# The three attention products in the order v, k, q, and the FFN's weight tiles shifted in steps of 16 bytes

## The chip, the core and the metric

The kernel runs on one core of a Trainium2 chip. The metric is device time in microseconds (us), the median of several executions. In a core, TensorE (PE) multiplies matrices, VectorE (DVE) and ScalarE (ACT) work element by element, GpSimd (POOL) does small vector work and issues some of the transfers, and SyncE (SP) issues most of the other transfers (DMAs). Each engine takes its instructions in its own order and waits on semaphores for the others. On PE each matmul needs its stationary operand loaded first; the profile lists that load as an instruction of its own, LDWEIGHTS, on a row PEld.

## What is computed

One layer of a streaming encoder, for 512 tokens of width 1024, in float32:

```python
h = rms_norm(x, norm_mix)
proj = h @ w_in                       # 8192 columns
u_pool, u_lru, q, k, v, g_logits = split(proj)
gates = sigmoid(g_logits + b_gate)    # three gates of 1024 columns
y_pool = pool_mixer(u_pool, ...); y_lru = rglru_mixer(u_lru, ...)
q = rms_norm(q per head, q_norm); k = rms_norm(k per head, k_norm)
y_sb = stick_breaking_attention(q, k, v)
merged = sum(gates[b] * (y[b] @ w_branch[b]) for b in range(3))
x = x + merged @ w_out
h2 = rms_norm(x, norm_ffn)
x = x + (silu(h2 @ w_ffn_gate) * (h2 @ w_ffn_up)) @ w_ffn_down   # 2816 wide
```

For this change it matters that q and k are normalised per head and that v is not.

## The kernel before

**Precision.** Each float32 operand is split into a high part, rounded to the matmul's format, and a low part, the rest. A product is then three matmuls: high by high, high by low, low by high. For weights, ACT writes the high part (a copy) and DVE the low part (a subtraction) of a tile of 128 x 1024; PE can't begin a product before both are there. `split_w` (lines 97 to 103) does it, with the tiles from `weight_tiles` (lines 93 to 95): tags `whi` and `wlo` of the pool `wp`, three buffers each. A weight tile has 1024 + 128 columns, of which a slice of 1024, beginning at column `o`, is used.

**Order.** The weight steps of the whole kernel, up to the FFN, stand in a list, `specs`, in the order in which PE will need them. `weights(key)` (lines 219 to 224) emits steps until up to three are ready, with a raised priority, so splits are made ahead of PE by as much as the three buffers allow. Work that follows a product (additions, norms, stores) goes to a list `bg`; `tick()` runs an entry of it after each part of a product.

**Startup** (lines 347 to 391). `WARM` small matmuls on a constant run on PE while the first data come. The small vectors `vt` are loaded by ACT's queue; the first tiles of x and the first halves of the first weight tile, `raw0`, are loaded by SP's queue in turn. Then PE multiplies the first gate columns (line 625).

**The stretch of q, k and v** (lines 718 to 765). Each of the three is a product of 512 tokens by 1024 columns with depth 1024, done by a scheme with seven block products in place of eight (`ORDER`: 11, 12, S2, S1, S3, S4, 22). Each block product is two halves of 12 matmuls with 512 moving columns (line 712), each with its own weight step of 128 x 1024. Eight of the fourteen weight steps of q, k or v also need a sum or difference of raw weight blocks on DVE (`qkv_sum`, line 150, by the table `SUMS_AT`). A snapshot (ACT, line 724) and an addition (DVE, line 727) make each of four result tiles, `r`, which `post` (lines 678 to 687) takes further. For q and k, `post` squares the tile (ACT, line 682), sums it per head (DVE, line 683) and puts `post2` on the list. `post2` (lines 689 to 701) computes the inverse root with `rsqrt` (lines 252 to 260: a power on POOL, then four small instructions on DVE), scales k's tile by it on ACT (eight copies, line 698) or, for q, writes the negated factor for later (line 700), and stores the tile with POOL's queue to the tensor `qd` in DRAM (line 675). For v, `post` only stores it.

The order is q (t = 0), k (t = 1), v (t = 2). Half chunks of the third gate, 24 matmuls each with one weight step, are placed after six of the block products by the table `AFTER`: after 12, S3 and 22 of q and after the same three of k. The last pieces of the recurrent mixer (inputs, scans and stores of its chunks 2 and 3, lines 601 to 614) are put on the list after q's S3.

After this stretch comes the pooling mixer together with the attention, head by head: `head_tasks` loads q, k and v of a head from `qd` by SP's queue (line 889), and PE transposes q and k (line 896).

**The FFN.** The first two of eleven chunks of the gate and up products are done directly, with 512 moving columns. The other nine (c = 2 to 10) use the seven-product scheme with 256 moving columns: each block product is 24 matmuls (`product`, lines 1176 to 1182). Six of eleven blocks of the down product are then done directly, and last come two halves of its output (c = 11 and 12) by the seven-product scheme again, 24 matmuls each block product. `make_a` (lines 1162 to 1174) makes the weight tiles for c = 2 to 12, three block products ahead. All of them lie at column `OFF` = 16 of their tile, so 64 bytes further in than the tiles of all other stages, which lie at column 0.

In the FFN the weight slice is the stationary operand and the activations are the moving one; in the stretch of q, k and v it is the other way round.

Of the kernel before, what the change touches and what calls it, by code (L numbers as in the profile page):

```python
# [25 lines left out]
QSCALE = float(HD) ** -0.5  # L26
NEG = -1.0e30
EARLY = 300
WARM = 8
GBUFS = 27  # L30
NDIRECT = 2
KD = 4
H = S // 2
AHEAD = 200
PAD = 96
OFF = 16
NAW, NAT, NAB = 8, 8, 13
NSP = 42
NLD = 12
# [24 lines left out]
def layer_kernel(ctx: ExitStack, tc: tile.TileContext, x, xt, vecs, w_in, w_pool, w_rg, w_ig,  # L64
                 w_branch, w_out, w_fg, w_fu, w_fd, out):
    nc = tc.nc
# [14 lines left out]
    def b4(shape, name, tag="b", dt=F32):  # L81
        bufs = {"w": NAW, "t": NAT, "b": NAB}[tag]
        return pools["ap0"].tile([P] + shape, dt, tag=tag, name=name, bufs=bufs)
# [5 lines left out]
    def cols(ap, k0, nk, c0, nc_):  # L89
        return ap[k0 * P:(k0 + nk) * P, c0:c0 + nc_].rearrange("(k p) c -> p k c", p=P)  # L90


    def weight_tiles(nh, nl, o=0):
        return [wp.tile([P, 1024 + 128], F32R, tag=tag, name=n)[:, o:o + 1024]
                for tag, n in (("whi", nh), ("wlo", nl))]
# [20 lines left out]
    def add_gate(br, c):  # L116
        add_chunk256(("gate", br, c), w_in, 5120 + br * 1024 + c * 256)
# [14 lines left out]
    WITH = {"11": "11", "12": "21", "S2": "T2", "S1": "T1", "S3": "T3", "S4": "22", "22": "T4"}  # L132
    CH = {"11": 0, "12": 0, "21": 1, "22": 1}
    KH = {"11": 0, "12": 1, "21": 0, "22": 1}
    qraw = {}

    def qkv_raw(t, nm, i):
        if (t, nm, i) not in qraw:
            qraw[t, nm, i] = r = b4([2, 512], f"qw{t}{nm}{i}", "w")
            nc.sync.dma_start(r, cols(w_in, 4 * KH[nm] + 2 * i, 2, 2048 + t * 1024 + CH[nm] * 512, 512))  # L140
        return qraw[t, nm, i]
# [15 lines left out]
    def add_seven(t, nm, i):  # L157
        def make(n):
            p = 2 * ORDER.index(nm) + i
            if p < 4:  # L160
                qkv_raw(t, nm, i)
            h, l = None, None
            if p == 1:
                h, l = split_w(qraw[t, nm, i], [P, 2, 512], n)
            if p in SUMS_AT:
                qkv_sum(t, *SUMS_AT[p])
            return (h, l) if h is not None else split_w(qraw[t, nm, i], [P, 2, 512], n)
        specs.append((("seven", t, nm, i), make))


    AFTER = {}
    for n, (t, nm) in enumerate(((0, "12"), (0, "S3"), (0, "22"), (1, "12"), (1, "S3"), (1, "22"))):
        AFTER[t, nm] = divmod(n, 2)

    for n in range(4):
        add_direct(("first", n), cols(w_in, 2 * n, 2, 5120, 512), 2, 512)
# [2 lines left out]
    for n in (0, 1, 2, 4, 3, 5, 6, 7):  # L179
        if n < 4:  # L180
            add_lru(n)
        else:
            add_gate(1, n - 4)
    for t in range(3):
        for nm in ORDER:
            add_seven(t, nm, 0)
            add_seven(t, nm, 1)
            if (t, nm) in AFTER:
                c, half = AFTER[t, nm]
                add_direct(("gate", 2, c, half), cols(w_in, 4 * half, 4, 7168 + c * 256, 256), 4, 256)  # L190
# [41 lines left out]
    vt = cst.tile([P, NV], F32, tag="vt", name="vt")  # L232
# [102 lines left out]
    with ExitStack() as first:  # L335
# [11 lines left out]
        wps = pb.tile([P, 2, S], F32, tag="mm", name="warm_ps")  # L347
        for i in range(WARM):
            nc.tensor.matmul(wps[:, 0, :], warm[:, 0:P], warm, start=True, stop=True)
# [7 lines left out]
        def load_xt(k):  # L357
            nc.sync.dma_start(xts[k], xt[k * P:(k + 1) * P, :])
# [12 lines left out]
        raw0 = wp.tile([P, 2, 512], F32, tag="raw", name="raw0")  # L371
        ready["first", 0] = hi0, lo0
        src0 = cols(w_in, 0, 2, 5120, 512)
        nc.scalar.dma_start(vt, vecs)
        for k in range(2):
            load_xt(k)
            nc.sync.dma_start(raw0[:, k, :], src0[:, k, :])
            dve.tensor_copy(hi0[:, k, :], raw0[:, k, :])
            dve.tensor_tensor(lo0[:, k, :], raw0[:, k, :], hi0[:, k, :].bitcast(F32), ALU.subtract)
            make_h(k)  # L380
# [239 lines left out]
        for k in range(KT):  # L620
            if k % 2 == 0:
                wh, wl = weights("first", k // 2)
# [51 lines left out]
        def store(t, i, j, r):  # L674
            nc.gpsimd.dma_start(rows(t, i, j), r)


        def post(t, i, j, r):
            if t < 2:
                sq = b4([2, 512], f"sq{t}{i}{j}")  # L680
                s_ = cst.tile([P, 8], F32, tag="ssq", name=f"ssq{t}{i}{j}", bufs=2)
                act(sq, r, AF.Square)
                dve.tensor_reduce(s_, sq.rearrange("p a (b d) -> p (a b) d", d=HD), AX.X, ALU.add)
                dve.tensor_scalar(s_, s_, 1.0 / HD, EPS, ALU.mult, ALU.add)
                bg.append(lambda: post2(t, i, j, r, s_))
            else:
                store(t, i, j, r)

        def post2(t, i, j, r, s_):

            y = cst.tile([P, 8], F32, tag="krs", name=f"krs{i}{j}", bufs=2) if t else \
                qrs[:, 0, 2 * j:2 * j + 2, 4 * i:4 * i + 4]
            y3 = y.rearrange("p (a b) -> p a b", a=2) if t else y
            rsqrt(y3, s_.rearrange("p (a b) -> p a b", a=2), (2, 4), f"q{t}{i}{j}")
            if t:
                v = r.rearrange("p a (b d) -> p (a b) d", d=HD)
                for n in range(8):
                    act(v[:, n, :], v[:, n, :], AF.Copy, scale=y[:, n:n + 1])
            else:
                dve.tensor_scalar(qrs[:, 1, 2 * j:2 * j + 2, 4 * i:4 * i + 4], y3, -1.0, None, ALU.mult)  # L700
            store(t, i, j, r)

        def tok_product(t, nm, ps, first):
            bh, bl = BQ[WITH[nm]]
# [10 lines left out]
                    tick()  # L715

        gate2 = {}
        for t in range(3):
            ps = {}
            r = {}  # L720

            def snap(key, src):
                r[key] = b4([2, 512], f"r{t}{key[0]}{key[1]}")
                act(r[key], src, AF.Copy)

            def final(key, src):
                dve.tensor_tensor(r[key], r[key], src, ALU.add)
                bg.append(lambda t=t, key=key, v=r[key]: post(t, *key, v))

            def bank(nm):  # L730
                ps[nm] = pb.tile([P, 2, 512], F32, tag="mm", name=f"ps_q{t}{nm}")
                return ps[nm]

            for nm in ORDER:
                if nm in ("11", "12", "S1", "22"):
                    bank(nm)
                dst = {"S2": "11", "S3": "11", "S4": "S1"}.get(nm, nm)
                tok_product(t, nm, ps[dst], dst == nm)
                if nm == "11":
                    snap((0, 0), ps["11"])  # L740
                elif nm == "12":
                    final((0, 0), ps["12"])
                elif nm == "S2":
                    snap((0, 1), ps["11"])
                elif nm == "S1":
                    snap((1, 1), ps["S1"])
                elif nm == "S3":
                    final((1, 1), ps["11"])
                    snap((1, 0), ps["11"])
                elif nm == "S4":  # L750
                    final((0, 1), ps["S1"])
                else:
                    final((1, 0), ps["22"])
                if (t, nm) == (0, "S3"):
                    for f, c in ((lru_input, 3), (lru_scan, 2), (lru_scan, 3), (lru_store, 2), (lru_store, 3)):
                        step(of(f, c))
                if (t, nm) in AFTER:
                    c, half = AFTER[t, nm]
                    if half == 0:
                        gate2[c] = chunk_psum(("gate", 2, c), pb)  # L760
                    half_chunk(gate2[c], ("gate", 2, c), half, hn, 1)
                    if half == 1:
                        gate_store(2, c, gate2[c], True)
# [258 lines left out]
    with ExitStack() as ffn:  # L1022
# [21 lines left out]
        for c in range(4):  # L1044
# [5 lines left out]
            for j in range(2):  # L1050
                k = 2 * c + j
                if c % 2 == 0:
                    x1p[c // 2, j] = mp.tile([P, 2, S], F32, tag="m", name=f"x1{c}{j}")
                t = x1p[c // 2, j][:, c % 2, :]
# [77 lines left out]
        CH = {"11": 0, "12": 0, "21": 1, "22": 1}  # L1132
        KH = {"11": 0, "12": 1, "21": 0, "22": 1}

# [4 lines left out]
        made = [0, NDIRECT]  # L1139

        def load_a(c):
            for nm in ("11", "21", "22", "12"):
                raw[c, nm] = t = corner([2, 4, P], f"w{c}_{nm}")
                for w in range(2):
                    if c < DOWN:
                        ap, c0 = (w_fg, w_fu)[w], c * 256
                    else:
                        ap, c0 = w_fd, (c - DOWN) * 512 + w * 256
                    nc.sync.dma_start(t[:, w], cols(ap, KH[nm] * 4, 4, c0 + CH[nm] * P, P))

# [11 lines left out]
        def make_a(upto):  # L1162
            while made[0] < min(upto, len(steps)):
                c, nm = steps[made[0]]
                made[0] += 1
                while made[1] < min(c + 2, DOWN):
                    load_a(made[1])
                    made[1] += 1
                sums_a(c, nm)
                h, l = (t.rearrange("p (w k c) -> p w k c", w=2, k=4)  # L1170
                        for t in weight_tiles(f"wh{c}_{nm}", f"wl{c}_{nm}", OFF))
                act(h, raw[c, nm], AF.Copy)  # L1172
                dve.tensor_tensor(l, raw[c, nm], h.bitcast(F32), ALU.subtract)  # L1173
                A[c, nm] = h, l
# [76 lines left out]
        for m in range(4):  # L1251
            t = fp.tile([P, 2, S], F32, tag="mm", name=f"ps_d{m}")
# [38 lines left out]
        for kc in range(KD, last + 1):  # L1291
            split_act(kc + 1)
            ah, al = split.pop(kc)
            for e in range(2):
                wh, wl = weights("fd", e, kc)
                if kc == last:
                    make_a(steps.index((DOWN, "11")) + e + 1)
                for j in range(4):
# [5 lines left out]
                    if kc == last:  # L1304
                        t = x1[m]
# [8 lines left out]
        for q in range(2):  # L1314
            c = DOWN + q
# [54 lines left out]
```

## Time and profile before

| | us |
|---|---|
| median of 3 executions | 939.15 |
| lowest, highest of them | 937.56, 939.16 |
| the profiled execution, its own time | 938.85 |
| its span, first to last instruction | 937.0 |

The profile gives busy time per engine, the chain of work that ended last, groups of instructions by line and shape, the waits and who ended them, and instructions in order of time. A row of the timeline has the start in us from the span's start, the duration in us (for a merged row the whole stretch), the engine, the line and the operation, and in brackets the idle time before it and who ended it. In the groups, the last two numbers ahead of the bar's right side are the total busy time in us and the mean duration of one in ns. In the windows, each row is a stretch of time; after its length come the busy time and, in brackets, the count of instructions of each engine, then the granted clock of TensorE as a share of the full one.

TensorE is busy for 99% of the span, VectorE for 76%, ScalarE for 52%. The mean granted clock is 0.998.

### The profile page before, as it was taken

How to read it: one execution, taken by the hardware profiler on the slowest of the kernel's cores; microseconds unless marked ns; L12 is line 12 of the kernel's file. 1: busy time of each engine (PE TensorE's matmuls, PEld its weight loads, DVE VectorE, ACT ScalarE, POOL GpSimd, SP SyncE). 2: the span in 40 equal slices, each digit the busy share in tenths (PEclk: the TensorE clock that was granted, in tenths of full speed). 3: DMA queues.
4: the chain of work that ended last, by engine and by line, in shares of the span. 5: the costliest groups of instructions: out<-in, count | busy, mean ns of one | idle time of the engine just before them, and what ended most of it. 6: DMA issues, size and time to landing. Idle time of an engine off the chain costs nothing.

```text
span 937.0 us, 13039 instructions
## 1 busy us (share of the span) xinstructions
PE 925.5 (99%) x5090; PEld 796.5 (85%) x5090; DVE 709.8 (76%) x890; ACT 489.6 (52%) x660; POOL 45.2 (5%) x69
## 2 busy tenths in 40 slices
PE   9999999899999999999999999999999999999998
PEld 6888778787878888788888888889999999988898
DVE  6797889777696699866865545699888888787465
ACT  6545997545655465644643234454554555653232
POOL 2000000222121000000000000000000000000000
PEclk9999999999999999999999999999999999999999
DMA  9484351652714934155532344355533334523001
GB/s 333 124 286 135 113 180 68 211 171 68 247 58 145 281 117 130 61 166 173 153 91 90 98 136 149 91 143 141 144 91 97 106 105 138 165 97 105 1 29 63
DMA packets 126894, 124.13 MB, mean 132 GB/s; under 512 B 7408, under 2 KB 105712, under 8 KB 126832
## 3 DMA queue, kind: packets, MB, share of 16 engines
q1 hardware_dynamic: 122800, 109.07, 38.2%
q0 software_dynamic: 3888, 14.16, 4.4%
q8 instruction: 40, 0.66, 0.3%
q14 instruction: 22, 0.18, 0.1%
q10 hardware_dynamic: 144, 0.06, 0.0%
HBM read 107.02 MB, written 16.25 MB: 132 GB/s over the span
## 4 chain that ended last, share of the span: by engine, by line
PE 82%; DVE 8%; ACT 5%; issue 3%; POOL 2%; DMA 0%; POOLq 0%; DVEq 0%; ACTq 0%
PE ps_y L1182 11%; PE ps_x L1182 8%; PE ps_br L227 5%; PE ps_br L229 5%; PE ps_br L228 5%; PE ps_q L712 3%; PE ps_d L227 3%; PE ps_d L228 3%; PE ps_d L229 3%; PE ps_gate L625 3%; PE ps_dy L1182 2%; DVE wlo L102 2%; PE ps_gate L227 2%; PE ps_gate L228 2%; PE ps_gate L229 2%
## 5 line engine op out<-in xcount | busy, mean ns | idle before, releaser
L101 ACT ACTIVATE whi<-raw 128x1024 fp32r<-128x1024 f32 x93 | 98.4, 1058 | 149.1 <-PE ps_br L228 46.2
L102 DVE TENSOR_TENSOR wlo<-raw,whi 128x1024 fp32r<-128x1024 f32 x93 | 113.5, 1221 | 63.8 <-ACT whi L101 58.6
L1172 ACT ACTIVATE wh_S<-w_S 128x1024 fp32r<-128x1024 f32 x44 | 46.6, 1061 | 56.6 <-PE ps_y L1182 25.6
L1173 DVE TENSOR_TENSOR wl_S<-w_S,wh_S 128x1024 fp32r<-128x1024 f32 x44 | 53.6, 1221 | 12.8 <-ACT wh_S L1172 12.6
L1172 ACT ACTIVATE wh<-w 128x1024 fp32r<-128x1024 f32 x33 | 35.0, 1062 | 49.0 <-issue 12.9
L102 DVE TENSOR_TENSOR wlo<-qw,whi 128x1024 fp32r<-128x1024 f32 x36 | 43.9, 1220 | 17.3 <-ACT whi L101 17.2
L1173 DVE TENSOR_TENSOR wl<-w,wh 128x1024 fp32r<-128x1024 f32 x33 | 40.3, 1222 | 17.4 <-ACT wh L1172 17.4
L101 ACT ACTIVATE whi<-qw 128x1024 fp32r<-128x1024 f32 x36 | 37.9, 1055 | 26.1 <-PE ps_q L712 17.6
L227 PE MATMUL ps_gate<-HH,whi 128*128 128x512 f32 x128 | 50.1, 392 | 0.0
L229 PE MATMUL ps_gate<-HH,wlo 128*128 128x512 f32 x128 | 49.9, 390 | 0.0
L228 PE MATMUL ps_gate<-HL,whi 128*128 128x512 f32 x128 | 49.8, 389 | 0.0
L227 PE MATMUL ps_d<-ah,whi 128*128 128x512 f32 x112 | 43.7, 391 | 0.0
L228 PE MATMUL ps_d<-al,whi 128*128 128x512 f32 x112 | 43.6, 389 | 0.0
L229 PE MATMUL ps_d<-ah,wlo 128*128 128x512 f32 x112 | 43.6, 389 | 0.0
L1160 DVE TENSOR_TENSOR w_S<-w,w 128x1024 f32<-128x1024 f32 x22 | 26.9, 1223 | 3.4 <-PE ps_d L228 2.9
L229 PEld LDWEIGHTS ps_gate<-HH,wlo 128*128 128x128 f32 x128 | 24.0, 188 | 5.3 <-DVE wlo L102 0.4
L227 PEld LDWEIGHTS ps_gate<-HH,whi 128*128 128x128 f32 x128 | 24.0, 188 | 5.2 <-issue 0.4
L228 PEld LDWEIGHTS ps_gate<-HL,whi 128*128 128x128 f32 x128 | 24.0, 188 | 4.9
L1160 DVE TENSOR_TENSOR w_S<-w,w_S 128x1024 f32<-128x1024 f32 x22 | 26.9, 1223 | 0.6
L933 DVE TENSOR_TENSOR_SCAN E<-K,zero 128x511 f32<-128x511 f32 (+3 forms) x32 | 25.5, 812 | 1.1 <-ACT K L928 1.1
L227 PE MATMUL ps_br<-yph,whi 128*128 128x512 f32 x64 | 25.6, 400 | 0.0
L227 PE MATMUL ps_pool<-HH,whi 128*128 128x512 f32 x64 | 25.6, 400 | 0.0
(634 smaller groups left out, 3015.7 us busy)
## 6 DMA issues: line engine op xcount, KB each, us to landing
raw<-in_w_in_dram SPq DMA_DIRECT2D x39, 512.0 KB, 4.9
qw<-in_w_in_dram SPq DMA_DIRECT2D x24, 512.0 KB, 4.7
raw<-in_w_branch_dram SPq DMA_DIRECT2D x24, 512.0 KB, 3.5
w<-in_w_ffn_gate_dram SPq DMA_DIRECT2D x36, 256.0 KB, 3.8
w<-in_w_ffn_up_dram SPq DMA_DIRECT2D x36, 256.0 KB, 4.2
raw<-in_w_ffn_down_dram SPq DMA_DIRECT2D x14, 512.0 KB, 3.5
qd<-r POOLq DMA_DIRECT2D x12, 512.0 KB, 3.4
at<-qd SPq DMA_DIRECT2D x24, 256.0 KB, 5.5
```

Of the source, the lines that this page charges most:

```text
L101: act(hi, raw, AF.Copy)
L102: dve.tensor_tensor(lo, raw, hi.bitcast(F32), ALU.subtract)
L227: nc.tensor.matmul(ps, lh, rh, start=start, stop=False, skip_group_check=skip)
L228: nc.tensor.matmul(ps, lh, rl, start=False, stop=False, skip_group_check=skip)
L229: nc.tensor.matmul(ps, ll, rh, start=False, stop=stop, skip_group_check=skip)
L625: nc.tensor.matmul(pss[n // 2][n % 2], w[:, k % 2, n * P:(n + 1) * P], hu[k][x_], start=k == 0 and w is wh and x_ == 0, stop=k == KT - 1 a ...
L712: nc.tensor.matmul(ps[:, a, :], b_[:, k, ts_], a_[:, kk, :], start=first and n == k == 0, stop=n == 2 and k == 3, skip_group_check=True)
L933: dve.tensor_tensor_scan(E[:, f - 1:c0 + n - 1][:, ::-1], K[:, f:c0 + n][:, ::-1], zero[:, 0:1].to_broadcast([P, c0 + n - f]), 1.0, ALU.mu ...
L1160: dve.tensor_tensor(t, raw[c, x], raw[c, y], op)
L1172: act(h, raw[c, nm], AF.Copy)
L1173: dve.tensor_tensor(l, raw[c, nm], h.bitcast(F32), ALU.subtract)
L1182: nc.tensor.matmul(o, a[:, w, k, :], b[:, k, :], start=first and n == k == 0, stop=n == 2 and k == 3, skip_group_check=True)
```

## The change

1. The three products run in the order v, k, q (`VKQ`), both in the list of weight steps and in the loop that issues the matmuls.
2. The half chunks of the third gate come after v's 12, S3 and 22, after k's 12, and after q's 11 and S2. The last pieces of the recurrent mixer come after v's S3.
3. `post` stores q's tile at once, like v's; only k's tile is stored in `post2`, after its scaling.
4. At the start `vt` is loaded by SP's queue, ahead of the first tile of x, and the first half of `raw0` by ACT's queue; `WARM` is 7 in place of 8.
5. In the FFN's seven-product parts the column at which a weight tile lies depends on the chunk and on the block product's place in it. For c = 3 to 6 it is 16 throughout, as before. For c = 2, 7, 8, 11 and 12 it is 0, 4, 8, 12, 16, 16, 16. For c = 9 and 10 it is 0, 124, 120, 116, 112, 112, 112. Four columns are 16 bytes.

```diff
-WARM = 8
+WARM = 7
...
-OFF = 16
+
+
+HELD, DOWNWARDS, UPWARDS = (16,) * 7, (0, 4, 8, 12, 16, 16, 16), (0, 124, 120, 116, 112, 112, 112)
+OFFS = {2: DOWNWARDS, 7: DOWNWARDS, 8: DOWNWARDS, 9: UPWARDS, 10: UPWARDS, 11: DOWNWARDS, 12: DOWNWARDS}
...
+    VKQ = (2, 1, 0)
...
-    for n, (t, nm) in enumerate(((0, "12"), (0, "S3"), (0, "22"), (1, "12"), (1, "S3"), (1, "22"))):
-        AFTER[t, nm] = divmod(n, 2)
+    for n, (t, nm) in enumerate(((0, "12"), (0, "S3"), (0, "22"), (1, "12"), (2, "11"), (2, "S2"))):
+        AFTER[VKQ[t], nm] = divmod(n, 2)
...
-    for t in range(3):
+    for t in VKQ:
         for nm in ORDER:
...
-        nc.scalar.dma_start(vt, vecs)
+        nc.sync.dma_start(vt, vecs)
         for k in range(2):
             load_xt(k)
-            nc.sync.dma_start(raw0[:, k, :], src0[:, k, :])
+            (nc.sync if k else nc.scalar).dma_start(raw0[:, k, :], src0[:, k, :])
...
-            else:
+            if t != 1:
                 store(t, i, j, r)
...
                     act(v[:, n, :], v[:, n, :], AF.Copy, scale=y[:, n:n + 1])
+                store(t, i, j, r)
             else:
                 dve.tensor_scalar(qrs[:, 1, 2 * j:2 * j + 2, 4 * i:4 * i + 4], y3, -1.0, None, ALU.mult)
-            store(t, i, j, r)
...
-        for t in range(3):
+        for t in VKQ:
...
-                if (t, nm) == (0, "S3"):
+                if (t, nm) == (VKQ[0], "S3"):
...
+                o = OFFS.get(c, HELD)[made[0] % 7]
...
-                        for t in weight_tiles(f"wh{c}_{nm}", f"wl{c}_{nm}", OFF))
+                        for t in weight_tiles(f"wh{c}_{nm}", f"wl{c}_{nm}", o))
```

## The prediction

> **What bounds the kernel now.** The page's first part comes first, then the windows view over the stretches that the change touches.
>
> ```profile
> PE 925.5 (99%) x5090; PEld 796.5 (85%) x5090; DVE 709.8 (76%) x890; ACT 489.6 (52%) x660; POOL 45.2 (5%) x69
> ```
>
> ```profile
> 148.57:207.39 58.82, 56.27 (x241) 46.16 (x240) 48.22 (x57) 30.86 (x33) 14.63 (x12) 0.97 0.54 179
> 207.39:263.18 55.79, 54.98 (x241) 44.90 (x240) 40.47 (x56) 31.75 (x45) 11.65 (x7) 1.00 0.42 132
> 263.18:301.84 38.66, 38.55 (x170) 31.31 (x168) 29.48 (x32) 22.40 (x35) 6.99 (x8) 1.00 0.29 100
> ...
> 148.57:176.90 28.33, 25.78 (x115) 21.03 (x113) 26.77 (x29) 17.12 (x19) 7.35 (x6) 1.00 0.38 130
> 176.90:180.40 3.50, 3.50 (x8) 2.79 (x9) 2.45 (x4) 0.00 (x0) 0.00 (x0) 0.51 0.86 264
> ```
>
> TensorE's own pace is the bound: it idles 11.5 us in all. The first three windows are q, k and v. They hold 2.55, 0.81 and 0.11 us of TensorE idle time, 3.5 together, and the last window a second loss: right after the longest wait, 8 matmuls took 3.5 us at a granted clock of 0.51. At full clock the spacing is:
>
> ```profile
> 605.92 0.39 PE L227 MATMUL ps_fu<-h2h,whi 128*128 128x512 f32 x1
> ...
> 616.80 0.39 PE L227 MATMUL ps_fg<-h2h,whi 128*128 128x512 f32 x1
> ```
>
> 48 matmuls lie between, so 10.88 / 48 = 0.2267 us each. Eight would take 1.81, so the low clock cost 1.7 us. All that a new order can win in q, k and v is thus 3.5 + 1.7 = 5.2 us. Who ended the waits, from the waits view of that stretch, and then the timeline up to the longest of them:
>
> ```profile
> DVE qrs L257 <- POOL rsqq L256: 6.4, 4, 1.8
> DVE krs L257 <- POOL rsqq L256: 5.3, 4, 1.9
> ...
> PE ps_q L712 <- DVE wlo L102: 2.5, 1, 2.5
> ...
> PE ps_q1S L712 <- DVE wlo L102: 0.8, 2, 0.5
> ```
>
> ```profile
> 165.81 1.19 DVE L683 TENSOR_REDUCE ssq<-sq 128x8 f32<-128x1024 f32 x1
> ...
> 168.31 3.69 POOL L256 TENSOR_TENSOR rsqq<-ssq,mhalf 128x8 f32<-128x8 f32 x1 [3.66 <-DVE ssq L684]
> ...
> 172.04 0.17 DVE L257 TENSOR_TENSOR qrs<-rsqq 128x8 f32<-128x8 f32 x1 [1.56 <-POOL rsqq L256]
> ...
> 173.31 1.22 DVE L610 TENSOR_TENSOR_SCAN li<-lt,ls 128x512 f32<-128x512 f32 x1
> ...
> 175.64 1.20 DVE L102 TENSOR_TENSOR wlo<-qw,whi 128x1024 fp32r<-128x1024 f32 x1
> ...
> 176.89 0.29 PEld L712 LDWEIGHTS ps_q<-wlo,hT3h 128*128 128x128 f32 x1 [2.97 <-DVE wlo L102]
> ```
>
> The reader is to see a queue on VectorE. The low weight part that TensorE wants stands behind the mixer's scans, and these behind an instruction of q's norm, L257, which holds VectorE idle for 1.56 us until POOL's power is done.
>
> **Part 1: v first.** v has no norm. Ahead of the wait at 176.9 VectorE then loses the reduction (1.19), the idle time (1.56) and the six small instructions of one norm. The small ones in that stretch, quoted by the 0.17 of L257, make about 6 x 0.17 = 1.0. Together 3.75 us, more than the 2.5 that TensorE waited. The scans stay where they were, after the first product's S3. So the wait goes, and with it the low clock behind it: -2.5 - 1.7 = **-4.2 us**. ScalarE also loses the square there. If only the scans decided, nothing would be gained; VectorE was busy 26.77 of 28.33 us in that window, so 3.75 us less is enough.
>
> The two waits of 0.8 us fall at k's S1, while VectorE still does q's last norms. Behind v there are none. I take half of it: **-0.4** (bounds -0.8 and 0).
>
> **Part 2: k and q with fewer gate chunks between.** A third of the stretch without gate halves is 38.55 us of TensorE for 168 matmuls (third window), and a gate half 24 x 0.2267 = 5.4. k keeps one of three: 38.6 + 5.4 = 44.0 us. VectorE's share, by the groups of k's window:
>
> ```profile
> L102 DVE TENSOR_TENSOR wlo<-qw,whi 128x1024 fp32r<-128x1024 f32 x12 | 14.7, 1222 | 7.3 <-ACT whi L101 7.3
> L683 DVE TENSOR_REDUCE ssq<-sq 128x8 f32<-128x1024 f32 x4 | 4.9, 1217 | 0.9 <-ACT sq L682 0.9
> ```
>
> 14 + 1 weight splits, 8 sums and 4 additions of the same 128 x 1024 size are 27 x 1.22 = 32.9; 4 reductions 4.9; 20 small ones at 0.17 3.4: 41.2 us. The waits on POOL add (6.4 + 5.3) / 8 x 4 = 5.9. 47.1 against 44.0: VectorE falls 3.1 us behind over k. What hides that is the lead: three weight buffers let it be two halves ahead, 2 x 12 x 0.2267 = 5.4 us, and in v's part it has 54.9 us of TensorE time for 17 splits, 8 sums, 4 additions (35.4) and about 10 of scans, so it enters k with the lead full. q then gets two gate halves near its beginning, 49.4 us for 41.2 + 1.2 + 0.7 + 5.9 = 49.0, level. The bounds are 0 (the lead covers it) and 3.1 + 1.7 = 4.8 (it doesn't, and one wait is long enough for the low clock). Bunched sums will cost something; I take **+0.8**, nearer the covered end, as k's window with as much of norms waited only 0.8.
>
> q last also puts q's norms ahead of the attention. Its stores no longer stand behind the norm (`post` issues them), but POOL is in order, so one can stand behind an earlier norm's power (3.69 us above at the longest). The first head's loads:
>
> ```profile
> 297.18 7.26 SPq L108 DMA_DIRECT2D raw<-in_w_in_dram  x3
> 304.61 1.48 SPq L889 DMA_DIRECT2D at<-qd  x3
> ```
>
> ```profile
> 296.31 0.73 POOL L675 DMA_DIRECT2D qd<-r  x1 [4.71 <-DVE r L727]
> ```
>
> SP's queue reaches them at 304.61 because of the weight loads ahead, over 8 us after the S4 result of the last third is stored now (296.31), so a store later by 3.7 us still lands. Bounds 0 and +2; I take **+0.2**. k's store moves past nothing, and v's and q's loads only change places in SP's queue with equal sizes.
>
> **Part 3: the start.**
>
> ```profile
> 0.74 0.40 ACTq L374 DMA_DIRECT2D vt<-in_vecs_dram  x1
> ...
> 0.74 0.40 SPq L358 DMA_DIRECT2D xt<-in_xt_dram  x1
> ...
> 1.19 0.44 SPq L377 DMA_DIRECT2D raw<-in_w_in_dram  x1
> ...
> 1.46 3.60 PE L349 MATMUL warm_ps<-warm 128*128 128x512 bf16 x8 [1.46 <-DVE warm L241]
> ...
> 3.92 0.72 ACT L364 ACTIVATE hu<-xt,vt 128x512 fp32r<-128x512 f32 x1 [1.16 <-DMA xt<-in_xt_dram]
> ...
> 5.35 0.42 DVE L378 CAST whi<-raw 128x512 fp32r<-128x512 f32 x1
> ...
> 5.91 2.05 PE L625 MATMUL ps_gate<-hu,whi 128*128 128x512 f32 x4 [0.86 <-DVE whi L378]
> ```
>
> x's first tile is issued 0.45 us later (behind `vt`), the weights 0.45 earlier. The first matmul waits for both; the cast ends at 5.77 and was itself behind VectorE's work on x. If the cast now goes ahead, the matmul starts up to 0.7 earlier; if not, 0.45 later. Those first matmuls are slow (4 in 2.05 us, against 0.91 at full pace), so an earlier start wins fewer full-pace matmuls than its length: **-0.2** (bounds -0.5 and +0.5). The eight warm-up matmuls end at 5.06, so one fewer ends ahead of the earliest start, 5.2.
>
> **Part 4: the FFN's offsets.** No transfer and no instruction is added; the same matmuls read from other columns.
>
> ```profile
> 638.72 2.83 PE ps_y L1182 x24
> ...
> 813.97 2.83 PE ps_y L1182 x24
> ```
>
> ```profile
> L228 PE MATMUL z<-qkl,qkh 128*128 128x256 f32 x16 | 4.7, 292 | 0.0
> L229 PE MATMUL py<-wth,vl 128*128 128x256 f32 x16 | 4.5, 284 | 0.0
> ...
> L228 PE MATMUL py<-wtl,vh 128*128 128x256 f32 x16 | 4.5, 282 | 0.0
> L229 PE MATMUL z<-qkh,qkl 128*128 128x256 f32 x16 | 4.5, 279 | 0.0
> ...
> L1182 PE MATMUL ps_y<-B011h,wh 128*128 128x256 f32 x5 | 1.4, 281 | 0.0
> ```
>
> A block product is 24 matmuls in 2.83 us, 117.8 ns each, and the chain shows this for every block product of c = 2 to 10. All of them hold 64 bytes of offset, so the rows say nothing of 0 to 48 bytes but this: z and py have the same width with no offset, and their mean durations are 279 to 292 ns against 281. 7 chunks have 4 block products at a new offset, 7 x 4 x 24 = 672 matmuls. Upper bound: + 11 ns x 672 = +7.4 us. Lower bound: half of a 512-column spacing, 113.3, so -4.5 x 672 = -3.0 us; and if the pace reached in steps then holds in all 1848 matmuls of this kind, -8.3. The nearest row, py, is 3 ns over for offset 0; between 0 and 64 bytes I take +1 ns on average, **+0.7**.
>
> The Trainium skill, page "TensorE: Matmul & The Clock Gate", Part 2, "Step-by-step: what each phase is for", says that the moving operand and the weight load come by two independent read ports, so that neither takes bandwidth from the other. By that rule the distance between them changes nothing, this term is 0 and the edit doesn't do what it says; the spread of 279 to 292 ns at one width is not decisive, since z and py also wait.
>
> **The sum** against the profiled execution's 938.85 (span 937.0, 1.85 around it): -4.2 - 0.4 + 0.8 + 0.2 - 0.2 + 0.7 = -3.1, so **935.8**; that execution lies 0.3 under the median of 939.15. Less than 0.2% of the time, 1.9 us, can't be told from no change.
>
> **The rivals.** (a) *A faster pace sets in with the steps.* For it: 117.8 is more than half of a 226.7 spacing, so there is something to lose per matmul. Against it: 1512 matmuls of c = 2 to 10 show one pace without exception, whatever precedes them. Time: 935.8 - 0.7 - 8.3 = 926.8, or 929.9 if only the seven stepped chunks have it (7 x 168 x 4.5 = 5.3). The same page, "Back-to-back issue gap", gives N / 2.4 + 2.5 ns for a single matmul, 109 ns here; by that estimate all 1848 would win 16 us, of which no row shows a sign. (b) *The intermediate offsets collide,* the other side. Place: the first four block products of the seven chunks; price 11 ns on 672 matmuls, +7.4, and +0.7 drops out: 942.5. It decides from 6 ns on (4.0 us over 672), where parts 1 to 3 are eaten up. For it: z's 292; against it: py's 282 to 284. (c) *VectorE can't carry k with one gate half.* Place: k's S3 to 22, where two gate halves are gone; price 4.8 us in place of 0.8: 939.8; a second such wait in q's last four products, where no gate half is left, 3 more: 942.8. For it: 47.1 against 44.0; against it: the lead of 5.4. (d) *v first doesn't remove the wait,* as the scans alone suffice to hold the weights back: 4.2 less gain, 940.0.
>
> **How the numbers follow.** Forecast 0.46 (933 to 938), (a) 0.20, (b) 0.14, (c) 0.12, (d) 0.08. Faster by over 0.2%, under 937.3: (a) and nine tenths of the forecast, 0.61. Within 0.2%: the rest of the forecast, two thirds of (d) and a part of (c), 0.14. Slower: 0.25. The range 927 to 942.5 leaves out the deepest of (a) and the far ends of (b) and (c), each below a tenth.
>
> **What would show it.** Part 1: no wait over 1 us on VectorE's `wlo` in the first third of the stretch, and a granted clock of 1.00 throughout. Part 2: waits on `wlo` under 1 us in all in k and q. Part 3: first matmul of line 625 at 5.2 to 5.9 us. Part 4: 2.83 us for 24 matmuls at 64 bytes, within 0.07 of it at the steps. The prediction is wrong if block products with HELD columns take another time than 2.83, if the clock drops in k or q, or if TensorE waits for q at the first transposes.

## The result and the profile after

| | before | changed |
|---|---|---|
| median, four executions each | 938.44 us | 926.89 us |
| lowest and highest | 937.56, 939.16 | 926.75, 929.27 |
| ratio, with its 95% interval | | 0.9883 (0.9864 to 0.9903) |
| profiled execution, its span | 938.85, 937.0 | 929.27, 927.1 |

Executions of either kernel differ by some 1.5 to 2.5 us with how fast the first dozen matmuls run (last section), so like is compared with like: when both were run again side by side, the lowest three are 937.10, 937.12 and 937.24 before, and 926.54, 926.72 and 926.73 changed, 10.4 to 10.6 us apart.

Where it came from, by windows cut at the first matmuls of the q, k, v stretch, of the nine FFN chunks and of the two down halves, and at the first matmuls that follow them (the prediction's windows of q, k and v begin 1.8 us later). The columns are the window, its length, then busy time and count of each engine, the granted clock, the DMA share and GB/s. First before:

```profile
146.76:300.02 153.26, 149.80 (x649) 122.37 (x648) 118.76 (x142) 86.70 (x113) 33.17 (x26) 0.99 0.42 139
638.56:816.64 178.08, 178.08 (x1514) 178.08 (x1513) 150.02 (x138) 97.55 (x120) 0.00 (x0) 1.00 0.41 119
890.24:932.64 42.40, 42.40 (x348) 41.76 (x347) 26.75 (x29) 12.74 (x12) 0.00 (x0) 1.00 0.10 36
```

The same after the change:

```profile
146.94:294.15 147.21, 147.21 (x650) 121.54 (x648) 115.89 (x129) 86.19 (x112) 23.01 (x24) 1.00 0.44 143
632.85:807.25 174.40, 174.40 (x1513) 174.40 (x1512) 149.60 (x138) 97.79 (x120) 0.00 (x0) 1.00 0.43 122
880.90:922.82 41.92, 41.92 (x349) 41.28 (x347) 26.77 (x29) 12.77 (x12) 0.00 (x0) 1.00 0.10 35
```

The stretch of q, k and v lost 6.05 us, the nine chunks 3.68, the down halves 0.48: 10.2 together. The spans differ by 9.9, so the other stages together take 0.3 longer. TensorE has no idle time left in the stretch, and the clock there is 1.00. In the FFN the count of matmuls is the same but for one at a window's edge, and TensorE was never idle before, so there the matmuls became cheaper.

VectorE's waits on POOL and TensorE's on weights in the stretch after the change, from the waits view (sum in us, times, longest):

```profile
DVE krs L261 <- POOL rsqq L260: 1.8, 1, 1.8
...
DVE qrs L261 <- POOL rsqq L260: 1.5, 1, 1.5
PEld ps_q2S L716 <- DVE wlo L105: 0.4, 1, 0.4
```

What were 2.5 and 0.8 us of TensorE's own waits is one weight load that came 0.4 late. VectorE's timeline where the long wait stood before:

```profile
164.90 1.23 DVE L614 TENSOR_TENSOR_SCAN li<-lt,ls 128x512 f32<-128x512 f32 x1
...
167.15 1.23 DVE L105 TENSOR_TENSOR wlo<-qw,whi 128x1024 fp32r<-128x1024 f32 x1
168.29 2.34 DVE L614 TENSOR_TENSOR_SCAN li<-lt,ls 128x512 f32<-128x512 f32 x2
170.54 1.21 DVE L105 TENSOR_TENSOR wlo<-qw,whi 128x1024 fp32r<-128x1024 f32 x1
171.65 1.23 DVE L614 TENSOR_TENSOR_SCAN li<-lt,ls 128x512 f32<-128x512 f32 x1
172.79 2.34 DVE L105 TENSOR_TENSOR wlo<-qw,whi 128x1024 fp32r<-128x1024 f32 x2
175.76 1.23 DVE L105 TENSOR_TENSOR wlo<-raw,whi 128x1024 fp32r<-128x1024 f32 x1 [0.63 <-ACT whi L104]
```

All four scans are still there, the last of them done at 172.88 in place of 175.72. The reduction and the wait for POOL are not, and the weight part that was begun at 175.64 is begun at 172.79. At the end VectorE is ahead: it waits for ScalarE.

The FFN in the chain of work that ended last (start, length, tile, count of matmuls), at c = 2, 6 to 7, and 9:

```profile
633.01 2.87 PE ps_y L1187 x24
635.88 2.84 PE ps_x L1187 x24
638.73 2.84 PE ps_y L1187 x24
641.56 2.83 PE ps_x L1187 x24
644.39 2.72 PE ps_y L1187 x24
...
723.27 2.72 PE ps_x L1187 x24
725.99 5.60 PE ps_y L1187 x48
731.59 2.84 PE ps_x L1187 x24
...
773.55 2.80 PE ps_y L1187 x24
...
779.15 2.83 PE ps_y L1187 x24
```

In c = 2 the four block products at new columns are slower than the 2.83 of before or level with it. Then, at the old column 16, the pace is 2.72, 113.3 ns a matmul in place of 117.8, and it lasts through c = 3 to 6, where nothing but the history differs from the kernel before. Going back to column 0 at c = 7 loses it for four block products; the upward way of c = 9 doesn't reach it at all: 2.80 at column 120, and 2.83 again at 112.

### The profile page after: what moved, and what is told of

Its sections match the earlier page's. It is cut to its first block, busy times and chain, and to the rows that moved or that the text cites. A ratio compares the mean times of both kernels' runs of the same rounds, so it can differ in the third digit from the quotient of the medians.

```text
span 927.1 us, 13041 instructions
## 1 busy us (share of the span) xinstructions
PE 919.4 (99%) x5089; PEld 791.8 (85%) x5089; DVE 709.2 (76%) x890; ACT 490.7 (53%) x660; POOL 38.3 (4%) x69
## 4 chain that ended last, share of the span: by engine, by line
PE 98%; DVE 1%; DMA 0%; issue 0%; ACT 0%; SPq 0%; DVEq 0%; ACTq 0%
PE ps_y L1187 11%; PE ps_q L716 9%; PE ps_x L1187 8%; PE ps_br L231 5%; PE ps_br L233 5%; PE ps_br L232 5%; PE ps_gate L231 4%; PE ps_gate L233 4%; PE ps_gate L232 4%; PE ps_d L231 3%; PE ps_d L233 3%; PE ps_d L232 3%; PE ps_gate L629 3%; PE ps_dy L1187 2%; PE ps_dx L1187 2%; PE ps_lru L231 2%
```

## The experiments

Where no ratio is given, the time is that of one execution, the profiled one.

**The two parts alone.** The offsets in the kernel before, and the changed kernel with column 16 everywhere:

```diff
-OFF = 16
+HELD, DOWNWARDS, UPWARDS = ...
+OFFS = ...
...
+                o = OFFS.get(c, HELD)[made[0] % 7]
```

> The kernel before with the changed table of offsets alone (order q, k, v, old start). If the two parts add up, it wins what the profiles show for the nine chunks and the two down halves: 178.08 - 174.40 and about 0.5, together 4.2 us, so 934.3 against 938.4. Rival: the pace of the FFN also depends on what went before it in the new order; then it is 938 or over, and block products stay at 2.83 us.

Measured: 933.28 us, ratio 0.9955 (0.9941 to 0.9968).

```diff
-OFFS = {2: DOWNWARDS, 7: DOWNWARDS, 8: DOWNWARDS, 9: UPWARDS, 10: UPWARDS, 11: DOWNWARDS, 12: DOWNWARDS}
+OFFS = {}
```

> The changed kernel with column 16 in all chunks, so the order v, k, q and the new start alone. If the parts add up: 926.9 + 4.2 = 931.1, every block product of the nine chunks at 2.83 us, the stretch of q, k and v at 147.2 us. Rival (the order needs the offsets): anything else.

Measured: 932.5 us, ratio 0.9938 (0.9924 to 0.9951). Its window of the stretch:

```profile
146.23:293.37 147.14, 147.14 (x649) 121.54 (x648) 115.87 (x129) 86.04 (x112) 22.97 (x24) 1.00 0.43 143
```

The block products stayed at 2.83 us. 0.45% and 0.62% add up to 1.07%, against 1.17% for both together: within the intervals the parts add up. The first gave the same sequence of 2.87, 2.84, 2.84, 2.83, 2.72 in the old order, so the FFN's pace doesn't hang on the order of q, k and v.

**Steps at c = 2 and c = 11 alone.** If the pace has a memory, the re-entries of c = 7 to 10 and 12 only cost.

```diff
-OFFS = {2: DOWNWARDS, 7: DOWNWARDS, 8: DOWNWARDS, 9: UPWARDS, 10: UPWARDS, 11: DOWNWARDS, 12: DOWNWARDS}
+OFFS = {2: DOWNWARDS, 11: DOWNWARDS}
```

> The changed kernel with the steps at c = 2 and c = 11 alone and column 16 in c = 3 to 10 and 12. Theory (the pace has a memory: reached by small steps it stays until the column jumps): all block products from the fifth of c = 2 on take 2.72 us, the nine chunks 63 x 2.72 + 0.5 = 171.9 us in place of 174.4, and c = 12 gains 0.5 more; 926.9 - 3.0 = 923.9. Rival (the fast pace wears off after some chunks, and the steps at 7 to 10 bring part of it back): block products of c = 7 to 10 at 2.83, time 927 or over.

Measured: 924.78 us, ratio 0.9862 (0.9847 to 0.9877). The window of the nine chunks:

```profile
632.25:804.11 171.86, 171.86 (x1514) 171.86 (x1512) 149.16 (x138) 97.63 (x120) 0.00 (x0) 1.00 0.43 124
```

171.86 as expected: after four block products at 2.83 to 2.87 all others take 2.72, for 160 us, through every other engine's work. The pace doesn't wear off. The run beside the changed kernel:

> The kernel with steps at c = 2 and c = 11 alone, beside the changed kernel on the same chip: 3.0 us less than that in executions with the same kind of start, as the windows of the nine chunks and the two down halves showed (171.9 against 174.4, and 0.5). Rival (it was the chip or the draw of executions): no difference over 1 us.

> The changed kernel once more: executions near 926.8 and near 929.2, by whether the first matmuls run at full pace; beside the kernel before, 10 us less in executions with the same kind of start.

Measured: 924.44 us, ratio 0.9855 (0.9837 to 0.9872), and for the changed kernel 926.73, 0.9884 (0.9864 to 0.9904). Its lowest two executions are 923.58 and 923.67, the changed kernel's 926.54 and 926.72: 3.0 us, as forecast from 2.5 in the nine chunks and 0.5 in c = 12. The two intervals overlap a little, but of its eight executions, four in each run, none is above the changed kernel's lowest of 926.54. This version beats both kernels.

**Other ways to column 16.**

```diff
+OFFS = {2: (0,) + (16,) * 6, 6: (0, 8) + (16,) * 5, 11: UPWARDS, 12: DOWNWARDS}
```

> The changed kernel with other ways to column 16: at c = 2 one jump from 0 to 16 after one block product, at c = 6 steps of 32 bytes (0, 8, 16), at c = 11 the upward way (0, 124 to 112) from the direct products, at c = 12 the steps of 16 bytes; all others hold 16. Theory (only small steps in the one direction reach the 2.72 pace): 2.83 after the jump through c = 5; c = 6 is open, 2.72 if 32 bytes is small enough; 2.80 to 2.83 at c = 11; 2.72 at the end of c = 12. Rival (it is enough to start from column 0): 2.72 after the jump too.

Measured: 931.06 us. From the chain, c = 2 with the jump, and the two down halves:

```profile
630.54 2.87 PE ps_y L1187 x24
633.41 2.83 PE ps_x L1187 x24
...
706.90 5.71 PE ps_y L1187 x48
712.61 2.84 PE ps_x L1187 x24
715.45 2.83 PE ps_y L1187 x24
...
896.66 2.82 PE ps_dy L1187 x24
...
913.70 2.95 PE ps_dx L1187 x24
916.65 2.73 PE ps_dy L1187 x24
```

The jump leads to 2.83 and stays there; so do steps of 32 bytes at c = 6 (the second half of the row at 706.90 and the two rows after it) and the upward way at c = 11. The last two rows are c = 12 at columns 12 and 16, where 16-byte steps bring the 2.72 pace even from the state that the upward way left. Column 12 itself took 2.95 there and 2.83 in the changed kernel's c = 2, so it too depends on the way. Of the four ways only the small steps in one direction work.

**A sweep over all columns.** Up by 4 with each block product to column 124, and back.

```diff
-                o = OFFS.get(c, HELD)[made[0] % 7]
+                n = made[0]
+                o = OFFS.get(c, HELD)[n % 7] if n > 62 else 4 * n if n < 32 else 4 * (63 - n)
```

> The changed kernel with a sweep in place of the table: block product n of the 63 of c = 2 to 10 lies at column 4 n up to 124 and then goes back by 4 each to 4; c = 11 and 12 take the steps and then hold 16. Theory (memory, the way matters): going up, 2.87, 2.84, 2.84, 2.83, then 2.72 from column 16 on for a while; going back, the same columns take other times than on the way up, 2.80 or 2.83 at some. Rival (each column has its pace, repeating every 32 columns): times are the same both ways, and 2.87 comes back at columns 32, 64 and 96.

Measured: 932.9 us. Three places of the chain, columns 16 and 20 on the way up, 80 and 84 on the way up (merged in one row), and 16 to 8 on the way back:

```profile
644.04 2.72 PE ps_y L1188 x24
646.76 2.85 PE ps_x L1188 x24
...
689.42 5.58 PE ps_y L1188 x48
...
800.19 2.83 PE ps_x L1188 x24
803.02 2.84 PE ps_y L1188 x24
805.86 2.84 PE ps_x L1188 x24
```

5.58 for the two fits the pair at columns 16 and 20, which takes 5.57, and the other block products at columns 64 to 124 agree with those at 0 to 60 to 0.01 us (merged rows as sums): the pattern on the way up repeats after 64 columns, 256 bytes, and not after 32 as the rival had it. On the way back column 16 (800.19) has 2.83 and no block product reaches 2.72. The range over all columns was 2.72 to 2.88. So column and way together set the pace. Column 16, with its repeat at 80, is the best place found, but only from below.

**The same for matmuls of 512 columns.** The weight steps of the third branch, the output projection and the first FFN chunks get columns 0 to 92, one step of 4 after the other.

```diff
-                  for t in weight_tiles("whi" + n, "wlo" + n))
+                  for t in weight_tiles("whi" + n, "wlo" + n, shift.get(int(n), 0)))
...
+    i0 = [key for key, _ in specs].index(("br", 2, 0, 0))
+    shift.update({i0 + m: 4 * m for m in range(24)})
```

> The kernel with steps at c = 2 and c = 11 alone, and in the direct products ahead of the FFN (third branch, output projection, first four FFN weight chunks: 24 weight steps of 24 matmuls of 512 columns) the column goes up by 4 with each weight step, from 0 to 92. If the 512-column matmuls have the same memory as the 256-column ones, their 5.44 us per step falls at some column, to 5.33 if they win the same 4.5 ns each. Rival (with 512 columns the weight load hides whatever the distance): 5.44 throughout.

Measured: 926.82 us. The window of the output projection, first in the kernel with the steps twice, then here:

```profile
544.60:588.12 43.52, 43.52 (x194) 36.05 (x193) 22.53 (x30) 15.94 (x21) 0.00 (x0) 1.00 0.45 145
```

```profile
543.81:588.27 44.46, 44.46 (x193) 36.07 (x192) 22.52 (x30) 15.95 (x21) 0.00 (x0) 1.00 0.44 142
```

Neither theory: the column matters with 512 columns as well, but on this way every change of it costs or is level. Columns 32 to 60, which the output projection passes through, are 0.94 us slower in its eight steps. Of the columns tried in these stages none was better than column 0.

**What the long wait hung on.** q's norm taken out of the kernel before:

```diff
+        nc.gpsimd.memset(qrs, 0.01)
         def post(t, i, j, r):
-            if t < 2:
+            if t == 1:
```

> The kernel before (q, k, v) without q's norm: q's square, reduction, power and the small instructions are left out, a constant stands in for the factor, and q is stored at once; the scans and the gate halves stay. Theory (q's norm on VectorE is what the long wait at 176.9 us hangs on): that wait and the low clock go, the two waits of k's S1 too, and the stretch falls from 153.3 to 147 to 148.5 us. Rival (the order itself or the places of the gate halves make the gain): it stays over 151.

Measured: 931.28 us, and the stretch:

```profile
144.90:292.54 147.64, 147.60 (x650) 121.39 (x648) 111.87 (x114) 82.82 (x109) 21.47 (x22) 1.00 0.44 144
```

147.64 in the old order, without q's norm, against 153.26 with it and 147.21 in the new order. The scans and the gate halves had stayed. So q's norm at that place was the loss, and the order v, k, q wins by moving it. Which part of the norm weighed most (the reduction, the wait for POOL, the square on ScalarE) these runs don't separate.

An earlier attempt from the other side missed its aim:

```diff
-                if (t, nm) == (0, "S3"):
+                if (t, nm) == (2, "S3"):
```

> The kernel before (q, k, v) with the last pieces of the recurrent mixer put on the list after v's S3 in place of q's. Theory (the long wait comes from q's norm and the mixer's scans meeting on VectorE): the wait at 176.9 us and the low clock behind it go, the stretch falls from 153.3 us by 4 or more, to 149 or under. Rival (the norms alone make the wait): it stays over 152.

Measured: 935.99 us, the stretch 152.03. The timeline shows why it says little on the scans:

```profile
170.33 0.17 DVE L257 TENSOR_TENSOR qrs<-rsqq 128x8 f32<-128x8 f32 x1 [1.56 <-POOL rsqq L256]
170.41 1.22 DVE L610 TENSOR_TENSOR_SCAN li<-lt,ls 128x512 f32<-128x512 f32 x1
...
172.79 1.22 DVE L610 TENSOR_TENSOR_SCAN li<-lt,ls 128x512 f32<-128x512 f32 x1
173.93 1.20 DVE L102 TENSOR_TENSOR wlo<-qw,whi 128x1024 fp32r<-128x1024 f32 x1
```

The scans stand where they stood: a later place in the list didn't move them. The long wait stayed too, and the 1.2 us by which the stretch is shorter are mostly those of k's two waits at S1, ahead of which one of POOL's powers took 2.50 us in place of 3.64; why it did isn't shown. Whether taking the scans away would also have been enough stays open.

**The gate halves at their old places,** in the first two thirds, with the order v, k, q and the steps twice:

```diff
-(0, "12"), (0, "S3"), (0, "22"), (1, "12"), (2, "11"), (2, "S2")
+(0, "12"), (0, "S3"), (0, "22"), (1, "12"), (1, "S3"), (1, "22")
```

> The kernel with steps at c = 2 and c = 11 alone, order v, k, q, but the six gate halves after 12, S3 and 22 of the first two products, v and k, so none in q. If VectorE's lead decides, q with 38.1 us of TensorE and some 49 of VectorE falls behind by more than the 5.4 of the lead, and the stretch of q, k and v grows from 147.2 to 150 or more. Rival (v first alone is the gain, the gate halves' places don't matter): 147.2 as in the changed kernel.

Measured: 927.43 us, and the stretch:

```profile
146.10:295.08 148.98, 147.96 (x650) 121.20 (x649) 116.35 (x129) 85.54 (x112) 24.79 (x24) 1.00 0.42 141
```

1.8 us over the changed kernel's stretch: less than expected, but not nothing as the rival had it. It is lost in q's part, and mostly at one place:

```profile
276.69 0.17 DVE L261 TENSOR_TENSOR qrs<-rsqq 128x8 f32<-128x8 f32 x1 [1.85 <-POOL rsqq L260]
...
277.54 1.22 DVE L105 TENSOR_TENSOR wlo<-qw,whi 128x1024 fp32r<-128x1024 f32 x1
```

```profile
278.81 0.50 PE L716 MATMUL ps_q<-wlo,hT3h 128*128 128x512 f32 x1 [0.95 <-DVE wlo L105]
```

It is the old mechanism again, a weight part behind q's norm and its wait for POOL. Of the 6.05 us of the stretch, 4.3 thus come without the new places of the gate halves and 1.8 hang on them.

**The old start** in the changed kernel.

```diff
-WARM = 7
+WARM = 8
...
-        nc.sync.dma_start(vt, vecs)
+        nc.scalar.dma_start(vt, vecs)
...
-            (nc.sync if k else nc.scalar).dma_start(raw0[:, k, :], src0[:, k, :])
+            nc.sync.dma_start(raw0[:, k, :], src0[:, k, :])
```

> The changed kernel with the start of before (small vectors by ACT's queue, first weights by SP's, 8 warm-up matmuls). Theory (the start wins about 0.7 us of waiting and, in some executions, an earlier full clock): 927.6 to 929.3, and its profile has the first matmul of the first gate at 5.9 us. Rival (the start is worth nothing): 926.9.

Measured: 928.71 us, ratio 0.9896 (0.9881 to 0.9912), overlapping the changed kernel's 0.9884 (0.9864 to 0.9904). The lowest execution is 926.82, against 926.54 for the changed kernel. The first matmul came at 5.84 us. The new start brings it 0.4 to 0.6 earlier (5.48 and 5.25 in two executions) and wins nothing that can be measured.

## Why the prediction was right and wrong

The direction was right and the size far too small: 935.8 forecast, 926.89 measured, 0.1 under the low end of the range. That this all but meets rival (a)'s 926.8 is chance: (a) had 8.3 us from the FFN and 3.8 from everything else, and measured were 4.2 in the FFN and 6.05 in q, k and v, and another 2.4 lie between the changed kernel's profiled execution (929.27) and its median. (Its other time, 929.9, should by its own terms be 929.8.) By the spans, with the same kind of start, the change is -9.9 us against a forecast of -3.1. Of the 6.8 between them, part 4 missed 4.9 and parts 1 and 2 together 2.4; the rest of the kernel missed 0.5 the other way.

**What bounds the kernel** held: each microsecond won was one in which TensorE waited or ran slowly.

**Part 1** named the right mechanism, as the run without q's norm shows. Its size was off. The loss to be won was put at 3.5 + 1.7 = 5.2 us and the stretch gave 6.05. The sum had only what the views call waits and the low clock. The matmuls around one wait of k's S1 before show the rest:

```profile
227.34 0.39 PE L712 MATMUL ps_q1S<-whi,hT1h 128*128 128x512 f32 x1
228.22 0.50 PE L712 MATMUL ps_q1S<-wlo,hT1h 128*128 128x512 f32 x1 [0.50 <-DVE wlo L102]
228.56 0.40 PE L712 MATMUL ps_q1S<-whi,hT1l 128*128 128x512 f32 x1
```

From start to start it is 0.88 and 0.34 us where 0.227 is normal: 0.77 us lost for a wait of 0.50. Counted in this way, by starts, the long wait and the slow matmuls behind it lost 4.4 us, where 4.2 were forecast; k's two waits lost 1.4, of which 0.4 were forecast; and two places in v's part lost 0.5, of which the prediction had 0.11 as idle time. The better bound was at hand, the length of the window less its matmuls at full pace: 153.26 - 648 x 0.2267 = 6.4 us.

**Part 2** forecast costs of 0.8 and 0.2; there were none. The bound of 0 came true, but not by the lead: the deficit of 3.1 us that the lead was to cover isn't there. The window of k's part, from its first matmul to q's:

```profile
201.67:245.19 43.52, 43.52 (x194) 36.04 (x192) 32.02 (x35) 25.82 (x32) 4.80 (x4) 1.00 0.41 133
```

VectorE is busy for 32.0 of 43.5 us, where 41.2 were forecast, and the waits on POOL there are 1.8 us, where 5.9 were. The forecast took 1.22 us for each of the large instructions, but they start 1.13 to 1.14 apart, and the window holds one reduction, one sum, one addition and some of the small instructions fewer than it counted. VectorE waits 7.9 us for ScalarE's high parts. The places of the gate halves did matter: at the old ones, with none in q, the stretch was 1.8 us longer. TensorE didn't wait at the first transposes.

**Part 3** had the first matmul at 5.2 to 5.9 (it was 5.25) and -0.2 us; the one is right, and of the other nothing could be measured.

**Part 4** is the step that failed: "between 0 and 64 bytes I take +1 ns on average, +0.7". It was -3.68 and -0.48, -4.2 us together. On the way from 0 to 12 the intermediate columns are indeed slower or level, 2.83 to 2.88, which is what the term priced. What it left out is that column 16 itself is faster when reached in this way, 2.72 in place of 2.83; that HELD columns take another time than 2.83 is what the prediction had named as a sign of being wrong. The rival (a) had that, with its price of 4.5 ns a matmul exact (117.8 to 113.3), and got 0.20. What was held against it, that 1512 matmuls show one pace, was no evidence: all of them had come to column 16 in the same way, by one jump. Of (a)'s two times neither shape was right, for the fast pace held in the unstepped chunks c = 3 to 6 and in the ends of c = 2, 7, 8, 11 and 12, and not in c = 9 and 10.

The rule of the Trainium skill weighed there (page "TensorE: Matmul & The Clock Gate", Part 2, "Step-by-step: what each phase is for") says that loading the next weights takes no read bandwidth from the running matmul. By that rule the column was to change nothing. In these runs 24 matmuls of one shape took 2.72 to 2.95 us by the weights' column and the way to it alone, and the measurement decides. Whether it is the two reads that get in each other's way isn't shown.

Rivals (b), (c) and (d) fell: the steps of the changed kernel cost at most 0.05 us a block product, k held, and the wait went.

## What to carry to other kernels

When TensorE is never idle, look at the pace of its matmuls: the spacing of starts in one stage against half or double the width in another can show whether there is something to win. The column at which the weights lie in their tile can change that pace, and so can the way in which it was reached; in a stage like this FFN, try steps of 16 bytes into a place, hold it, and don't jump away. For what stalls cost, take a window's length less its matmuls at full pace, not the sum of the waits.

## What the runs showed of the hardware

The pace of the FFN's matmuls with 256 columns has a memory. At one and the same placement it was 117.8 ns after a jump and 113.3 after four 16-byte steps, each for as long as the placement was held (up to 59 block products, 160 us). The pattern over the columns on the way up repeats after 256 bytes, and is another on the way back. What keeps the memory isn't shown by any run here, nor whether it is the weights' own place that counts or their distance from the moving operands, which no edit moved.

Executions of one kernel differ in its first matmuls. First the changed kernel's profiled execution above, then a later execution of it:

```profile
5.25 2.08 PE L629 MATMUL ps_gate<-hu,whi 128*128 128x512 f32 x4 [0.62 <-ACT hu L368]
```

```profile
5.48 1.20 PE L629 MATMUL ps_gate<-hu,whi 128*128 128x512 f32 x4 [0.86 <-ACT hu L368]
```

The same four matmuls take 2.08 or 1.20 us, and the second execution's first q, k, v matmul comes at 144.65 in place of 146.94 us. In the first execution the next four start 0.43 us apart (7.13 to 8.83 us), as the matmuls did before the change right after the long wait, where the granted clock was 0.51. But here the profile gives a granted clock of 1.00 in both executions, so that the clock is the cause isn't shown.

The Trainium skill, page "TensorE: Matmul & The Clock Gate", Part 1, "What's actually happening", says that the window by which the clock is released runs freely, so that the moment of release varies from run to run. The two kinds of start fit that, but the granted clock of 1.00 doesn't bear it out. Neither the number of warm-up matmuls (7 or 8) nor the order of the first loads removed the difference: with 8 and the old order, the first four took 2.05 us in the profile before and 1.16 in the run without q's norm.
